# Differential attention in a hybrid diffusion step: both softmax maps kept with queries on partitions, blended there and transposed on TensorE

## The chip, the cores and the metric

The kernel runs on one core of one Trainium2 chip. The metric is the device time of one execution in microseconds (us); the time before is the median of three runs. One more execution was recorded by the hardware profiler, and all rows below come from that one.

## What is computed (the reference, cut)

Two layers run over 640 tokens (512 latent tokens and 128 context tokens) of width 1024. Each layer projects its input once, gives the parts to three groups of heads (grouped-query attention, differential attention, a gated recurrence), and multiplies the gated results with one output matrix, followed by a layer norm. The change concerns the differential heads: 4 heads of width 64, each with two softmax maps over key width 32. Latent queries see 640 keys (128 cached, 512 latent); context queries see 128.

```python
def diff_attention(q, k, v, lam):
    scale = DIFF_QK_DIM ** -0.5
    def block(qb):
        s = jnp.einsum('bqhmd,bkhmd->bhmqk', qb, k).astype(jnp.float32) * scale
        p = jax.nn.softmax(s, axis=-1)
        a = p[:, :, 0] - lam * p[:, :, 1]
        return jnp.einsum('bhqk,bkhd->bqhd', a.astype(v.dtype), v)
    return _merge_blocks(lax.map(block, _query_blocks(q)))
# in the layer:
o_d = rms_norm(diff_attention(d_q, kd, vd, lam), subln) * (1.0 - lam_init)
out_d = o_d.reshape(b, n, DIFF_WIDTH) * jax.nn.silu(d_g)
```

## The kernel before

A layer has two parts. In the first, a Python scheduler (`drive`) weaves several streams into one program order: the input projections are the background (`bg_stream`: 14 chunks of 256 columns in the order of `ORDER`, with small modulation products between them as `MODS` says), and six foreground streams go ahead of it in the order of `PRIO` whenever they are ready. Each `yield` of a stream names a cost, as TensorE time and latency, from the table `COST`; the scheduler only uses it to choose the order. In the second part the output projection and the layer norm run.

Projections are split into high and low halves (three products for one) of type float32r; their outputs are written to a pool of 49 buffers of 128x640 float32 (`gran`, `GRAN = 49`), which nearly all large tiles of the layer share. PSUM is divided into banks by use: two for projections (A), three for transposed scores, transposes and small things (B), one for attention outputs (O), and one double bank for forward scores (S).

The attention heads go through three foreground streams. `prep_stream` (`diff_prep`, L1104) rotates, transposes and splits queries and keys, and lays them out by DMA as operand tiles `QD` and `KD` of 96 rows for one map of one head; `ahead` and the constant `LOOK` limit how far it may run ahead. `sp_stream` (L639) makes the forward pass `s_pass` (L1010) for two items at a time, where an item is one map of one head: for each of 4 query tiles, scores with queries on partitions into the S bank (L1023), the row maximum on VectorE (L1030), the exponential in place with the row sum on ScalarE (L1031). Only the maximum and the sum are kept: `finish_m` makes one offset for each row, a small product turns it (L1039), and ScalarE writes it into additional rows of the query operand (L1042). `SPA` limits how many passes run ahead of the values. `pv_stream` (L650) then computes the scores again, transposed, with keys on partitions (`st_tile`, L1082, the offset included as additional rows of the contraction), takes the exponential (L1088), and multiplies the result with the values (`pv_steps`, L1146; plain float32, two heads beside each other in the output's rows). For the differential heads this is done for map 0 and for map 1, and VectorE blends the two outputs (L1166). The 128 context queries take the same way in `s_ctx`, `st_ctx` and `diff_pv_ctx` (L1168). The grouped-query heads use the same functions with `two=True`.

The recurrence (`hgrn_pair`) copies blocks of its matrices out of PSUM, those of width 32 on ScalarE (L925) and those of width 64 on VectorE (L927).

Of the kernel before, what the change touches and what calls it, by code (L numbers as in the profile page):

```python
# [39 lines left out]
LOOK = (0, 1)  # L40
PEND = 0
SPA = (2, 3)
# [5 lines left out]
COST = (dict(mod=(0.43, 2.59), norm0=(0.0, 4.0), norm1=(0.4, 0.96), gmix=(0.35, 21.63), h_exp=(0.06, 2.01),  # L48
              h_diag=(2.13, 0.37), h_lvl=(0.0, 3.0), h_mm=(0.99, 0.0), h_kst=(0.0, 1.4), h_tr=(0.0, 0.0),
              h_u=(7.96, 1.11), h_out=(22.66, 1.86), s_max=(0.0, 1.59), s_tr=(0.0, 0.2), c_max=(0.44, 3.0),  # L50
              c_tr=(1.29, 0.0), d_rq=(0.0, 1.96), d_rk=(0.53, 1.34), d_spl=(0.77, 1.91), d_tr=(4.22, 0.0),
              d_ctx=(0.72, 1.8), pv_c=(0.3, 0.3), g_ss=(0.0, 1.28), g_rope=(0.0, 2.5), g_k=(0.0, 0.71),
              g_ctx=(0.0, 1.2), g_spl=(0.0, 0.87), g_tr=(1.22, 2.24), pv_c2=(4.13, 5.2), s_g=(0.49, 1.79),
              s_d=(0.38, 1.88), pv_e=(0.77, 0.7), pv_g=(1.3, 0.56), pv_d=(1.04, 0.21)),
        dict(mod=(1.04, 9.27), norm0=(0.36, 5.34), norm1=(0.0, 0.68), gmix=(0.15, 21.63), h_exp=(0.0, 1.75),
              h_diag=(1.09, 1.27), h_lvl=(0.0, 3.0), h_mm=(0.89, 0.0), h_kst=(0.0, 1.63), h_tr=(0.0, 0.0),
              h_u=(7.96, 1.11), h_out=(22.66, 2.33), s_max=(0.3, 1.59), s_tr=(0.0, 0.19), c_max=(0.36, 3.68),
              c_tr=(1.29, 0.0), d_rq=(0.0, 1.96), d_rk=(0.53, 1.34), d_spl=(0.72, 1.39), d_tr=(2.29, 0.0),
              d_ctx=(0.6, 1.8), pv_c=(0.0, 0.28), g_ss=(0.0, 1.28), g_rope=(1.04, 4.49), g_k=(0.0, 0.71),
              g_ctx=(0.0, 1.2), g_spl=(0.07, 0.35), g_tr=(1.22, 2.24), pv_c2=(4.13, 5.4), s_g=(0.34, 2.27),  # L60
              s_d=(0.37, 1.67), pv_e=(0.77, 0.97), pv_g=(1.3, 0.44), pv_d=(0.86, 1.01)))
# [12 lines left out]
def hybrid_kernel(ctx: ExitStack, tc: tile.TileContext, A, cst, outs):  # L74
# [36 lines left out]
    def bankB():  # L111
        return bank("B")
# [410 lines left out]
    def layer(l, hT, first, defer):  # L523
# [115 lines left out]
        def sp_stream():  # L639
            for j in range(8):  # L640
                yield lambda: j < SPA[l] or ("pv", j - SPA[l]) in done
                yield from s_pass(2 * j, items, prog, j >= 4)
                done.add(("sp", j))
                if j % 2:
                    yield from s_ctx(2 * j - 2, items, j >= 4)
                    done.add(("spc", j))
# [3 lines left out]
        def pv_stream():  # L650
            for j in range(8):
                yield has(("sp", j))
                it = items[2 * j:2 * j + 2]
                if j < 4:
                    if j % 2 == 0:
                        outs[j] = outs[j + 1] = gran(name="of")
                    yield from diff_pv(l, j % 2, it, nlam, outs[j])
                else:
                    outs[j] = gran(name="mf")
                    yield from gqa_pv(j // 2 - 2, it, outs[j])  # L660
                done.add(("pv", j))
                if j % 2:
                    yield has(("spc", j))
                    it = items[2 * j - 2:2 * j + 2]
                    if j < 4:
                        yield from diff_pv_ctx(l, it, nlam, outs[j])
# [175 lines left out]
    def hgrn_pair(l, p, q, G, Kk, rv, out):  # L842
# [167 lines left out]
    def s_pass(n0, items, prog, two):  # L1010
        nmx = small.tile([128, 4, 2], F32, tag="nmx", name="nmx")
        den = small.tile([128, 4, 2], F32, tag="den", name="den")
        K1 = slice(0, 128) if two else slice(0, 96)
        off = 64 if two else 96
        for i in range(2):
            yield lambda: len(items) > n0 + i
            it = items[n0 + i]
            for t in range(4):
                ps = bankS()
                ql = it["q1"][K1, 128 * t:128 * t + 128]  # L1020
                for h in range(2):
                    c = slice(320 * h, 320 * h + 320)
                    mm(out=ps[:, h, 0:320], lhsT=ql, rhs=it["k1"][K1, c], start=True, stop=not two)  # L1023
                if two:
                    for h in range(2):
                        c = slice(320 * h, 320 * h + 320)
# [428 lines left out]
```

## Time and profile before

| | before |
|---|---|
| median of 3 runs | 952.72 us (952.4 to 954.18) |
| the profiled execution, as timed | 954.79 us |
| its span, first to last instruction | 953.0 us |
| TensorE, matmul busy | 901.2 us (95%) |
| VectorE busy | 596.5 us (63%) |
| ScalarE busy | 582.1 us (61%) |
| GpSimd busy | 79.3 us (8%) |
| attention part of layer 0, output part, attention part of layer 1 (about) | 75 to 438, 438 to 520, 520 to 890 us |

Busy is the time in which at least one instruction of the engine runs; matmuls are pipelined, and one starts while the one before it still drains. In the rows, PE is TensorE, PEld its weight loads, DVE VectorE, ACT ScalarE, POOL GpSimd, SPq the queue that issues DMAs; L1023 is line 1023 of the kernel before. Tiles are named as in the program (pS, pB, pO, pA are PSUM banks).

### The profile page before, as it was taken

How to read it: one execution, taken by the hardware profiler on the slowest of the kernel's cores; microseconds unless marked ns; L12 is line 12 of the kernel's file. 1: busy time of each engine (PE TensorE's matmuls, PEld its weight loads, DVE VectorE, ACT ScalarE, POOL GpSimd, SP SyncE). 2: the span in 40 equal slices, each digit the busy share in tenths (PEclk: the TensorE clock that was granted, in tenths of full speed). 3: DMA queues.
4: the chain of work that ended last, by engine and by line, in shares of the span. 5: the costliest groups of instructions: out<-in, count | busy, mean ns of one | idle time of the engine just before them, and what ended most of it. 6: DMA issues, size and time to landing. Idle time of an engine off the chain costs nothing.

```text
span 953.0 us, 20559 instructions
## 1 busy us (share of the span) xinstructions
PE 901.2 (95%) x8213; PEld 749.7 (79%) x8213; DVE 596.5 (63%) x1340; ACT 582.1 (61%) x1309; POOL 79.3 (8%) x113
## 2 busy tenths in 40 slices
PE   6999999999999999999999999999989989999995
PEld 3798877887777758678989997878768867777895
DVE  2355557756777865343697466785587795544467
ACT  2335677567776867773265368656877676877311
POOL 0000002000001010200023000020000100210012
PEclk8899999999999999999999999999999999999998
DMA  9946521344431212215614452114124122114222
GB/s 291 315 139 177 150 88 37 104 138 112 128 92 53 91 32 69 70 51 186 208 67 151 114 153 86 29 45 120 51 78 122 47 69 54 51 45 133 77 91 99
DMA packets 103617, 100.37 MB, mean 105 GB/s; under 512 B 9449, under 2 KB 91873, under 8 KB 103521
## 3 DMA queue, kind: packets, MB, share of 16 engines
q1 hardware_dynamic: 103520, 99.05, 35.0%
q8 instruction: 65, 1.06, 0.5%
q14 instruction: 32, 0.25, 0.1%
HBM read 77.25 MB, written 6.31 MB: 88 GB/s over the span
## 4 chain that ended last, share of the span: by engine, by line
PE 70%; DVE 12%; ACT 7%; DMA 7%; issue 2%; SPq 1%; POOL 0%; DVEq 0%; ACTq 0%; POOLq 0%
PE pA L373 8%; PE pA L375 8%; PE pA L374 8%; PE pO L1146 7%; PE pA L394 5%; PE pS L1023 5%; PE pA L395 5%; PE pA L396 5%; DMA wraw<-in_w_in_dram 4%; DMA Q<-Q 2%; PE pS L1027 2%; PE pB L1082 2%; PE pB L1080 2%; PE pB L1079 2%; ACT pS L1031 1%
## 5 line engine op out<-in xcount | busy, mean ns | idle before, releaser
L1030 DVE TENSOR_REDUCE nmx<-pS 128x1 f32<-128x640 f32 x128 | 105.4, 823 | 119.9 <-PE pS L1023 65.3
L373 PE MATMUL pA<-wh,mh 128*128 128x256 f32 x600 | 171.0, 285 | 1.3 <-DVE gate_t L409 1.3
L375 PE MATMUL pA<-wh,ml 128*128 128x256 f32 x600 | 170.3, 284 | 0.0
L374 PE MATMUL pA<-wl,mh 128*128 128x256 f32 x600 | 170.0, 284 | 0.0
L1031 ACT ACTIVATE pS<-pS,nmx 128x640 f32<-128x640 f32 x128 | 98.2, 767 | 50.4 <-DVE nmx L1030 47.5
L260 ACT CAST wh<-wraw 128x512 fp32r<-128x512 f32 x140 | 83.7, 619 | 73.4 <-PE pA L375 31.9
L261 DVE TENSOR_TENSOR wl<-wraw,wh 128x512 fp32r<-128x512 f32 x140 | 92.8, 689 | 39.8 <-ACT wh L260 39.0
L373 PEld LDWEIGHTS pA<-wh,mh 128*128 128x128 f32 x600 | 114.7, 191 | 3.6 <-DVE gate_t L409 2.0
L375 PEld LDWEIGHTS pA<-wh,ml 128*128 128x128 f32 x600 | 114.6, 191 | 1.7 <-issue 1.2
L374 PEld LDWEIGHTS pA<-wl,mh 128*128 128x128 f32 x600 | 114.7, 191 | 1.1 <-issue 0.8
L1088 ACT ACTIVATE PT<-pB 128x512 f32<-128x512 f32 x160 | 89.1, 599 | 27.0 <-PE pB L1080 14.7
L394 PE MATMUL pA<-mh,wh 128*128 128x320 f32 x224 | 71.6, 320 | 0.0
L394 PE MATMUL pA<-hh,wh 128*128 128x320 f32 x224 | 70.6, 315 | 0.7 <-DVE gate_t L409 0.7
L395 PE MATMUL pA<-ml,wh 128*128 128x320 f32 x224 | 70.8, 316 | 0.0
L396 PE MATMUL pA<-mh,wl 128*128 128x320 f32 x224 | 70.6, 315 | 0.0
L396 PE MATMUL pA<-hh,wl 128*128 128x320 f32 x224 | 69.7, 311 | 0.0
L395 PE MATMUL pA<-hl,wh 128*128 128x320 f32 x224 | 69.5, 310 | 0.0
L1146 PE MATMUL pO<-PT,tk 128*64 128x512 f32 x256 | 64.9, 613 | 0.4 <-ACT PT L1088 0.3
L373 PE MATMUL pA<-wh,hh 128*128 128x256 f32 x200 | 57.6, 288 | 0.0
L375 PE MATMUL pA<-wh,hl 128*128 128x256 f32 x200 | 57.0, 285 | 0.0
L374 PE MATMUL pA<-wl,hh 128*128 128x256 f32 x200 | 56.8, 284 | 0.0
L394 PEld LDWEIGHTS pA<-mh,wh 128*128 128x128 f32 x224 | 43.2, 193 | 2.5 <-issue 1.8
(297 smaller groups left out, 1966.3 us busy)
## 6 DMA issues: line engine op xcount, KB each, us to landing
wraw<-in_w_ada_dram SPq DMA_DIRECT2D x32, 512.0 KB, 4.5
wraw<-in_w_in_dram SPq DMA_DIRECT2D x30, 512.0 KB, 4.6
wraw<-in_w_in_dram SPq DMA_DIRECT2D x48, 256.0 KB, 3.4
wa<-in_w_ada_dram SPq DMA_DIRECT2D x32, 256.0 KB, 5.4
wraw<-in_w_out_dram SPq DMA_DIRECT2D x16, 512.0 KB, 3.5
Q<-Q SPq DMA_DIRECT2D x32, 160.0 KB, 2.6
KD<-dkh SPq DMA_DIRECT2D x32, 96.0 KB, 3.2
QD<-dqh SPq DMA_DIRECT2D x32, 80.0 KB, 3.2
```

The lines of the kernel that those rows point to most:

```text
L260: nc.scalar.copy(hi[n], src)
L261: tt(out=lo[n], in0=src, in1=hi[n].bitcast(F32), op=ALU.subtract)
L373: mm(out=ps[:, o:o + 256], lhsT=hi[k][:, sl], rhs=a, start=(n == 0), stop=False)
L374: mm(out=ps[:, o:o + 256], lhsT=hi[k][:, sl], rhs=b, start=False, stop=False)
L375: mm(out=ps[:, o:o + 256], lhsT=lo[k][:, sl], rhs=a, start=False, stop=(n == last))
L394: mm(out=ps, lhsT=wa, rhs=hi[k][:, sl], start=(k == 0), stop=False)
L395: mm(out=ps, lhsT=wa, rhs=lo[k][:, sl], start=False, stop=False)
L396: mm(out=ps, lhsT=wb, rhs=hi[k][:, sl], start=False, stop=(k == KB - 1))
L1030: dve.tensor_reduce(out=nmx[:, t, i:i + 1], in_=sv, axis=AX.XY, op=ALU.max, negate=True)
L1031: act(sv, sv, AF.Exp, bias=nmx[:, t, i:i + 1], accum_out=den[:, t, i:i + 1])
L1088: return pt, act(pt, ps, AF.Exp).ins
L1146: x = mm(out=o[64 * (i % 2):64 * (i % 2) + 64], lhsT=value(k, i % 2), rhs=pt, start=k == 0, stop=k == 4)
```

## The change

The differential heads no longer compute their scores twice. `d_pass` takes both maps of one head: scores with queries on partitions as before, but the exponential is written to a kept tile `P` of 128x640 in SBUF. For each query tile map 1 is scaled by the row factor -lambda x (sum of map 0) / (sum of map 1) and added to map 0 on VectorE. When both heads of a pair are blended, `turn_maps` transposes the blended map in 128x128 blocks on TensorE, ScalarE copies four of them out of PSUM at a time, and the values are multiplied once for each head. The remaining factor, 1 / (sum of map 0) for each query, is broadcast, transposed likewise, and multiplied onto the output. The context queries go the same way (`d_ctx`, `diff_pv_ctx`). The additional rows of the operands, their memsets and the writes of turned maxima are dropped for these heads; the grouped-query heads keep theirs. The recurrence's 64-wide blocks are copied on ScalarE too. The constants of the scheduler (`LOOK`, `SPA`, `PRIO`, `ORDER`, `MODS`, `COST`) are set anew; the changes of `COST` are left out here.

```diff
-LOOK = (0, 1)
+LOOK = (1, 2)
-SPA = (2, 3)
+SPA = (3, 5)
...
-PRIO = ((1, 0, 2, 3, 5, 4), (0, 5, 1, 2, 3, 4))
-ORDER = ((0, 1, 4, 3, 2, 5, 6, 8, 7, 9, 10, 11, 12, 13),
-         (0, 1, 3, 2, 4, 5, 7, 6, 8, 9, 10, 11, 12, 13))
+PRIO = ((2, 3, 4, 1, 0, 5), (0, 5, 1, 2, 3, 4))
+ORDER = ((0, 1, 4, 3, 2, 5, 6, 7, 8, 9, 10, 11, 12, 13),
+         (1, 0, 3, 4, 2, 5, 7, 6, 8, 9, 10, 11, 12, 13))
...
-        {0: (8,), 3: (9,), 9: (10,), 10: (11,)})
+        {2: (8,), 3: (9,), 9: (10,), 10: (11,)})
...
-                yield from s_pass(2 * j, items, prog, j >= 4)
+                yield from s_pass(2 * j, items, prog) if j >= 4 else d_pass(2 * j, items, prog, nlam)
...
             for j in range(8):
+                if j in (0, 2):
+                    continue
                 yield has(("sp", j))
-                it = items[2 * j:2 * j + 2]
+                it = items[4 * (j // 2):4 * (j // 2) + 4]
                 if j < 4:
-                    if j % 2 == 0:
-                        outs[j] = outs[j + 1] = gran(name="of")
-                    yield from diff_pv(l, j % 2, it, nlam, outs[j])
+                    outs[j - 1] = gran(name="of")
+                    yield from diff_pv(it, outs[j - 1])
+                    done.add(("pv", j - 1))
...
-                        if m == 32:
-                            nc.scalar.copy(o, v[r])
-                        else:
-                            dve.tensor_copy(o, v[r])
+                        nc.scalar.copy(o, v[r])
...
+    def map_tile(it, t, den):
+        ps = bankS()
+        for h in range(2):
+            mm(out=ps[:, h, 0:320], lhsT=it["q1"][0:96, 128 * t:128 * t + 128],
+               rhs=it["k1"][0:96, 320 * h:320 * h + 320], start=True, stop=True)
+        nmx = small.tile([128, 1], F32, tag="nmd", name="nmd", bufs=4)
+        sv = ps[:, :, 0:320]
+        dve.tensor_reduce(out=nmx, in_=sv, axis=AX.XY, op=ALU.max, negate=True)
+        P = gran(name="P")
+        act(P.rearrange("p (h k) -> p h k", h=2), sv, AF.Exp, bias=nmx, accum_out=den)
+        return P
+
+    def d_pass(n0, items, prog, nlam):
+        den = small.tile([128, 2, 4], F32, tag="dend", name="dend", bufs=2)
+        rd = small.tile([128, 2, 4], F32, tag="rdd", name="rdd", bufs=4)
+        rat = small.tile([128, 4], F32, tag="rat", name="rat")
+        yield lambda: len(items) > n0 + 1
+        maps = []
+        for t0 in (0, 2):
+            late = []
+            for t in (t0, t0 + 1):
+                maps.append(map_tile(items[n0], t, den[:, 0, t:t + 1]))
+                yield cost["s_d"]
+                late.append(map_tile(items[n0 + 1], t, den[:, 1, t:t + 1]))
+                yield cost["s_d"]
+            ts = slice(t0, t0 + 2)
+            dve.reciprocal(rd[:, :, ts], den[:, :, ts])
+            stt(out=rat[:, ts], in0=rd[:, 1, ts], scalar=nlam, in1=den[:, 0, ts], op0=ALU.mult, op1=ALU.mult)
+            for t, b in zip((t0, t0 + 1), late):
+                stt(out=maps[t], in0=b, scalar=rat[:, t:t + 1], in1=maps[t], op0=ALU.mult, op1=ALU.add)
+            prog[0] = n0 + 1 + t0 // 2
+        items[n0].update(maps=maps, rd=rd[:, 0])
+        yield cost["s_max"]
...
+    def turn_maps(maps):
+        ps = bankB()
+        n = 128 * len(maps)
+        for i, x in enumerate(maps):
+            nc.tensor.transpose(ps[:, 128 * i:128 * i + 128], x, ident)
+        pt = gran((128, n), name="PT")
+        return pt, nc.scalar.copy(pt, ps[:, 0:n]).ins
...
-            yield ahead(4 * p + n)
-            i = 2 * (n % 2) + n // 2
-            r = slice(32 * i, 32 * i + 32)
+            yield ahead(4 * p + n - n % 2)
+            r = slice(32 * n, 32 * n + 32)
...
-            nc.gpsimd.memset(it["k1"][96:104].bitcast(F32), 1.0)
...
+    def diff_pv(items, of):
         dv, cv = items[0]["v"]
+        pair = (items[0], items[2])
+        rb = gran((128, 4, 2, 64), name="rb")
+        for e, it in enumerate(pair):
+            nc.scalar.copy(rb[:, :, e], it["rd"].unsqueeze(2).to_broadcast([128, 4, 64]))
+        ps = bankC()
+        for t in range(4):
+            nc.tensor.transpose(ps[:, 128 * t:128 * t + 128], rb[:, t].rearrange("p e d -> p (e d)"), ident)
+        r = gran((128, 512), name="rows")
+        nc.scalar.copy(r, ps)
         o = bankO()
...
+        def made(e, kt):
+            return turn_maps([x[:, 128 * kt:128 * kt + 128] for x in pair[e]["maps"]])
+
+        yield from pv_steps(made, value, o, "pv_d")
+        tt(out=of[:, 0:512], in0=o, in1=r, op=ALU.mult)
```

`d_ctx` does for the 128 context queries what `map_tile` and `d_pass` do for the others (four exponentials into one tile `P`, two small blends), and `diff_pv_ctx` transposes two blocks and one broadcast of row factors for each pair of heads, multiplies with the values of both heads, and scales.

## Rows read from the trace of the kernel before

**Rows 1.** The page's engine line: busy us (share of the span) xinstructions.
```profile
PE 901.2 (95%) x8213; PEld 749.7 (79%) x8213; DVE 596.5 (63%) x1340; ACT 582.1 (61%) x1309; POOL 79.3 (8%) x113
```

**Rows 2.** Table of stretches: stretch, its length, busy us by engine, granted clock, DMA.
```profile
75.00:438.00 363.00, 348.92 (x3329) 275.66 (x3329) 226.17 (x476) 251.92 (x566) 26.96 (x36) 1.00 0.34 97
110.00:270.00 160.00, 153.84 (x1572) 122.20 (x1572) 106.19 (x226) 108.28 (x247) 11.32 (x17) 1.00 0.37 103
520.00:890.00 370.00, 355.51 (x3350) 293.42 (x3350) 232.83 (x468) 254.91 (x570) 25.81 (x36) 0.99 0.29 82
```

**Rows 3.** The chain that ended last, by engine (the page's part 4).
```profile
PE 70%; DVE 12%; ACT 7%; DMA 7%; issue 2%; SPq 1%; POOL 0%; DVEq 0%; ACTq 0%; POOLq 0%
```

**Rows 4.** TensorE's waits: waiter <- releaser: us in total, times, longest.
```profile
PE pB L1067 <- DVE mhc L1008: 3.8, 3, 1.6
...
PE pO L1146 <- ACT PT L1088: 0.5, 2, 0.3
```

**Rows 5.** Timeline, two forward score tiles in a row: start us, length us, instruction.
```profile
90.33 0.46 PE L1023 MATMUL pS<-KD,QD 96*128 96x320 f32 x2
...
92.63 0.56 PE L1023 MATMUL pS<-KD,QD 96*128 96x320 f32 x2
```

**Rows 6.** TensorE's groups by shape: xcount | busy us, mean ns | idle before.
```profile
L1082 PE MATMUL pB<-QD,KD 100*128 100x512 f32 x80 | 30.5, 430 | 2.8 <-ACT PT L1088 1.9 <-ACT QD L1042 0.6
...
L1101 PE MATMUL pB<-cs,tk 128*128 128x128 f32 x90 | 14.7, 279 | 0.4 <-DVE tk L448 0.3
```

**Rows 7.** TensorE's timeline: transposed scores (L1082) and values (L1146) among projections.
```profile
118.57 1.00 PE L1082 MATMUL pB<-QD,KD 100*128 100x512 f32 x3
119.41 0.28 PE L375 MATMUL pA<-wh,hl 128*128 128x256 f32 x1
...
119.89 0.39 PE L1082 MATMUL pB<-QD,KD 100*128 100x512 f32 x1
120.12 0.28 PE L373 MATMUL pA<-wh,hh 128*128 128x256 f32 x1
...
120.80 1.08 PE L1146 MATMUL pO<-PT,dcv 128*64 128x512 f32 x4
121.71 1.03 PE L1146 MATMUL pO<-PT,tk 128*64 128x512 f32 x4
122.67 0.56 PE L1023 MATMUL pS<-KD,QD 96*128 96x320 f32 x2
```

**Rows 8.** TensorE's timeline: context scores (L1055) and turned maxima (L1039).
```profile
247.58 0.23 PE L1055 MATMUL pS<-KD,QD 96*128 96x128 f32 x1
247.69 0.41 PE L1039 MATMUL pB<-identr,mhl 128*4 128x128 f32 x4
247.93 0.49 PE L1055 MATMUL pS<-KD,QD 96*128 96x128 f32 x3
```

**Rows 9.** TensorE's timeline: four transposes of 128x128 float32 and the next instruction.
```profile
790.35 0.60 PE L961 MATMUL pB<-cs,kst 128*128 128x128 f32 x4
790.78 0.27 PE L965 MATMUL pB<-cs,kst 128*128 128x128 f32 x1
```

**Rows 10.** ScalarE's groups: exponentials of transposed scores, writes of turned maxima.
```profile
L1088 ACT ACTIVATE PT<-pB 128x512 f32<-128x512 f32 x160 | 89.1, 599 | 27.0 <-PE pB L1080 14.7 <-PE pB L1082 11.4
...
L1042 ACT ACTIVATE QD<-pB,cs 4x512 fp32r<-4x512 f32 x16 | 10.1, 671 | 7.4 <-PE pB L1039 7.3
```

**Rows 11.** VectorE's groups: row maxima, 64-wide block copies, a blend-like product of 128x640.
```profile
L1030 DVE TENSOR_REDUCE nmx<-pS 128x1 f32<-128x640 f32 x128 | 105.4, 823 | 119.9 <-PE pS L1023 65.3 <-PE pS L1027 54.0
...
L927 DVE COPY af<-pB 64x320 f32<-64x320 f32 x16 | 7.8, 487 | 2.2 <-PE pB L904 1.9
...
L568 DVE SCALAR_TENSOR_TENSOR sq<-of,sgain,sq 128x640 f32<-128x640 f32 x4 | 3.5, 881 | 1.9 <-ACT sq L567 1.9
```

**Rows 12.** Waits of the DMA queue: L94 moves query and key rows into tiles.
```profile
SPq L94 <- DVE kst L954: 14.8, 1, 14.8
```

More of the change, by code (lines that the diff above doesn't have):

```diff
@@ L1019, in s_pass @@
                 ps = bankS()
-                ql = it["q1"][K1, 128 * t:128 * t + 128]
+                ql = it["q1"][:, 128 * t:128 * t + 128]
                 for h in range(2):
                     c = slice(320 * h, 320 * h + 320)
[L1023 to L1026, printed above, removed]
-                        mm(out=ps[:, h, 0:320], lhsT=it["q2"][0:72, 128 * t:128 * t + 128], rhs=it["k2"][0:72, c],
-                           start=False, stop=True)
+                    mm(out=ps[:, h, 0:320], lhsT=ql, rhs=it["k1"][:, c], start=True, stop=False)
+                for h in range(2):
+                    c = slice(320 * h, 320 * h + 320)
+                    mm(out=ps[:, h, 0:320], lhsT=it["q2"][0:72, 128 * t:128 * t + 128], rhs=it["k2"][0:72, c],
+                       start=False, stop=True)
                 sv = ps[:, :, 0:320]
@@ L1031, in s_pass @@
                 act(sv, sv, AF.Exp, bias=nmx[:, t, i:i + 1], accum_out=den[:, t, i:i + 1])
-                yield cost["s_g" if two else "s_d"]
+                yield cost["s_g"]
             prog[0] = n0 + i + 1
@@ L1054, in s_ctx @@
             q, q2, k1, k2 = it["q1"][:, 512:640], it["q2"][:, 512:640], it["k1"][:, 640:768], it["k2"][:, 640:768]
-            mm(out=o, lhsT=q[K1], rhs=k1[K1], start=True, stop=not two)
-            if two:
-                mm(out=o, lhsT=q2[0:72], rhs=k2[0:72], start=False, stop=True)
+            mm(out=o, lhsT=q, rhs=k1, start=True, stop=False)
+            mm(out=o, lhsT=q2[0:72], rhs=k2[0:72], start=False, stop=True)
         dve.tensor_reduce(out=nmx, in_=ps[:, 0].rearrange("p (i k) -> p i k", i=4), axis=AX.X, op=ALU.max,
@@ new lines, in d_ctx @@
+    def d_ctx(n0, items, nlam):
+        nmx = small.tile([128, 4], F32, tag="nmxc", name="nmxc")
+        den = small.tile([128, 4], F32, tag="denc", name="denc")
+        rat = small.tile([128, 4], F32, tag="ratc", name="ratc")
+        yield lambda: len(items) > n0 + 3 and "ctx" in items[n0]
+        ps = bankS()
+        for i, it in enumerate(items[n0:n0 + 4]):
+            mm(out=ps[:, 0, 128 * i:128 * i + 128], lhsT=it["q1"][0:96, 512:640], rhs=it["k1"][0:96, 640:768],
+               start=True, stop=True)
+        dve.tensor_reduce(out=nmx, in_=ps[:, 0].rearrange("p (i k) -> p i k", i=4), axis=AX.X, op=ALU.max,
+                          negate=True)
+        P = gran((128, 4, 128), name="P")
+        for i in range(4):
+            act(P[:, i], ps[:, 0, 128 * i:128 * i + 128], AF.Exp, bias=nmx[:, i:i + 1], accum_out=den[:, i:i + 1])
+        dve.reciprocal(rat, den)
+        for i in range(0, 4, 2):
+            stt(out=rat[:, i + 1:i + 2], in0=rat[:, i + 1:i + 2], scalar=nlam, in1=den[:, i:i + 1], op0=ALU.mult,
+                op1=ALU.mult)
+            stt(out=P[:, i], in0=P[:, i + 1], scalar=rat[:, i + 1:i + 2], in1=P[:, i], op0=ALU.mult, op1=ALU.add)
+        items[n0]["ctx"] = (P, rat)
+        yield cost["c_max"]
@@ L1136, in diff_prep, with pv_steps @@
         out[-4]["ctx"] = True
-    def pv_steps(items, two, value, o):
+    def pv_steps(made, value, o, key):
         ready = []
         for kt in range(6):
-            now = [st_tile(items[e], kt, two) for e in range(2)] if kt < 5 else []
+            now = [made(e, kt) for e in range(2)] if kt < 5 else []
             if len(ready) == 4 or kt == 5:
@@ L1151, in pv_steps @@
             ready += now
-            yield cost["pv_e" if kt == 5 else "pv_g" if two else "pv_d"]
-    def diff_pv(l, m, items, nlam, of):
+            yield cost["pv_e" if kt == 5 else key]
+    def diff_pv(items, of):
         dv, cv = items[0]["v"]
+        pair = (items[0], items[2])
[7 more added lines that the diff above has]
+        nc.scalar.copy(r, ps)
         o = bankO()
```

92 lines of the change are left out of this document (41 added, 51 removed).

## The prediction

> **What bounds the kernel now.** I read the engine line of the page first: TensorE is busy in 95% of the span, ScalarE and VectorE in 61 and 63% [rows 1]. That is a mean over stages, so the table of stretches comes next. The change touches only the attention part of the two layers, 75 to 438 us and 520 to 890 us; there too TensorE is busy 348.9 of 363 us and 355.5 of 370 us, 96% of both, VectorE 62 and 63% [rows 2]. The reader is to see that the projections of the same layer fill whatever the attention leaves of TensorE. The chain that ended last says the same: 70% of it is TensorE work, 12% VectorE [rows 3]. And TensorE's own waits are short; of those around the attention heads, the worst is the wait of the small product that transposes the context maxima, 3.8 us in 3 waits; the value products waited for their exponentials 0.5 us in all [rows 4]. So in these stretches a matmul that goes away is time, if the next chain has room. The next chain is the score chain: one PSUM buffer, so scores, row maximum, exponential, then the next scores. Its period is 92.63 - 90.33 = 2.30 us [rows 5]; 128 tiles of it are 294 us out of 733 us of attention. It has room for more than twice its length.
>
> **How TensorE is priced.** The duration of a matmul in the groups is its latency, because matmuls overlap: 279 ns for a transpose, 430 ns for a 512-column score product [rows 6]. What it costs a full engine is the distance from its start to the next start. Three score products start at 118.57 and the next instruction at 119.41: 0.28 us each; a single one takes 120.12 - 119.89 = 0.23, and I take 0.25. Four records of the value product (two heads, two records each, since the operands are plain float32) take 121.71 - 120.80 = 0.91 and then 122.67 - 121.71 = 0.96 us: 0.93 for one key tile of two heads [rows 7]. The four small products that turn the maxima take 247.93 - 247.69 = 0.24, or 0.06 each; a context score product of 128 columns 247.69 - 247.58 = 0.11 [rows 8]. Four transposes of 128x128 float32 take 790.78 - 790.35 = 0.43, or 0.108 each [rows 9].
>
> **What TensorE loses.** In two layers there are 8 passes over a differential map pair, each with 10 transposed score products: 80 [rows 6], all gone: 80 x 0.25 = 20.0 us. The context's 16 transposed ones of 128 columns, at the 0.11 of the forward one, 1.8 us [rows 8]. The values are multiplied with one blended map instead of two, so 4 of 8 runs of 5 key tiles go: 20 x 0.93 = 18.6 us. The 32 small products that turn the maxima: 1.9 us; those of the context and half of the context's value products, about 1 us together. Sum removed: 43.3 us.
>
> **What it gains.** Each pair of heads now needs, for 5 key tiles, 2 heads and 4 query tiles, 40 transposes; 2 pairs and 2 layers make 160. The row factors are broadcast and transposed as well: 4 for each pair, 16; the context has 2 + 1 for each pair, 12. Together 188 x 0.108 = 20.3 us. The forward score products stay as they are. Net: 43.3 - 20.3 = 23 us less TensorE work.
>
> On that price one rule speaks against the change. In the trace a group of four transposes occupies TensorE for 0.43 us although each lasts 279 ns, so they overlap [rows 6, 9]. The Trainium skill ("TensorE: Matmul & The Clock Gate", Part 4, PE-mode transpose) gives about 275 ns for one transpose in a kernel and says that transposes don't hold the clock up. By 275 ns the 188 would take 52 us and the sum would turn into +8 us; the latency agrees with the trace, the price in a stream does not.
>
> **Waits.** Gone with the maxima: the context wait of the differential heads. Two of the 3 waits are theirs; the third, the longest at 1.6 us, belongs to the grouped-query heads, so 2.2 us go [rows 4]. New: the first transposes of a pair wait for the last blend, that is two products of 0.88 and some small reciprocals on VectorE behind the last exponential [rows 11], about 2.5 us of latency. Projection matmuls stand beside it and cover most; the trace of before has no such wait, so it is bounded by 0 (all covered) and 2.5 us x 4 pairs = 10 us (nothing covered). I take 4, nearer to the covered end, since the same kind of wait, exponential to value product, is covered but for 0.5 us now [rows 4]. So 23 + 2.2 - 4 = 21 us are gained.
>
> **The other engines.** ScalarE: 80 exponentials of 599 ns become 40 copies of the same shape out of PSUM, -24 us; the 16 writes of turned maxima go, -10; four copies of the output go, about -3; added are broadcast and row copies, some +6, and the 16 copies of the 64-wide recurrence blocks that come over from VectorE, at no more than their 0.49 there, +7 [rows 10, 11]. Net about -24 of 582 us. VectorE: 32 blends of 128x640 at 0.88 are +28 us [rows 11], the context's blends and reciprocals some +6; gone are the 16 block copies (-7.8) and the arithmetic on maxima and masks, about -10. Net +16 of 596 us: 64% busy, still no bound. Queued behind the blends on VectorE are the next row maximum and the low halves of the projection weights. A pass of 8 score tiles gets 4 blends, 3.5 us on 18.4 us, so the score chain grows to at most 2.7 us a tile in these stretches, and is still half of the time that it has. GpSimd loses 16 memsets and is idle anyway. The DMAs that lay out queries and keys are the same number in the same queue; they may start earlier (the look-ahead is one tile longer), and the keys' buffers come free after the forward pass instead of after the values.
>
> The retuned order of chunks moves work between neighbours but neither adds nor removes any; I cost it at nothing, covered by the fact that TensorE has something to do in 96% of either order. If that cover is gone, the price is that of a stall of a projection for a weight load, a few us.
>
> **Rivals.**
> 1. The handover binds. Both heads of a pair must be blended before the first transpose, so the value products of a pair come later and in one block of 10 steps, and the blends stand in VectorE's line. Then the uncovered end of the new wait holds (10 us in place of 4), and the score chain's growth, 64 differential tiles x 0.4 = 26 us, shows in perhaps a fifth, 5 us: 952.7 - 21 + 6 + 5 = 943. For it: the row maximum waits 65 us in total for differential and other score products already, so the two run in lockstep [rows 11]. Against: TensorE rarely waits for either of them.
> 2. More waits go than I count. TensorE idles some 28 us in the two attention parts together [rows 2]; a lighter ScalarE, fewer handovers and one pass over the values could return a third of that: 952.7 - 21 - 10 = 922.
> 3. Slower: the pool of 49 large buffers runs out. The blended maps are kept as 128x640 tiles: 8 for a pair until its values are done, up to 4 more for the next head and 4 second maps in flight, where before only 4 exponential tiles were live at once; 4 query tiles a pair come free earlier, so some 8 to 10 more of 49. That the pool is short now is visible: moves into query tiles waited 14.8 us for a buffer that the recurrence held [rows 12]. If the projections' outputs have to wait for a buffer until a pair is done, TensorE stops, since there are two PSUM banks for them. One stop would last about a run of values, 12 us; four of them make 48, and 952.7 - 21 + 48 = 980. It decides against the change from 5.3 us a pair on (21 / 4). Against: no wait of TensorE in the trace ends on such a release.
> 4. Slower: transposes don't overlap in their new place (they come behind blends and between float32 products), and cost their 279 ns [rows 6]: 188 x 0.279 = 52 us, net 52 - 43 = +9, and with the waits of the sum above +11: 964. The page of the Trainium skill named above ("TensorE: Matmul & The Clock Gate", Part 4) gives nearly that figure. Against it stand the four in 0.43 us, and the clock: the stretch from 110 to 270 us, which holds 22 transposes in such groups, ran at a granted clock of 1.00 [rows 2].
> 5. The change does less than it says: schedule and savings cancel within 0.2%, 952.
>
> **How the numbers follow.** The profiled execution took 953.0 us in its span and 954.8 as timed, 2 us above the median of 952.7; less 21 that execution would be 933.6, and against the median it is 931.5; I give 931. Chances: forecast 0.62 (926 to 937), rival 1 0.13, rival 2 0.12, rival 3 0.08, rival 4 0.02, rival 5 0.03. The range for 8 in 10 takes in rivals 1 and 2 with a margin for the bounds of the new wait: 916 to 946. A measurement of this kernel can tell about 0.2% (2 us) from no change: faster 0.87, same 0.03, slower 0.10.
>
> **What would show it.** Right: the transposed score products of the differential heads are gone, 80 fewer records of value products, some 188 transposes whose groups of four stand 0.43 us apart, TensorE's busy time down by over 20 us at an unchanged 95% share, VectorE up by about 16 us and ScalarE down by about 24. Rival 1 would show as idle time of TensorE before the map transposes, released by VectorE; rival 3 as projection matmuls that wait for an evacuation which waits for a buffer; rival 4 as groups of four that take over 1 us, or as a lower granted clock in 110 to 270 us and 570 to 725 us. The prediction is wrong if TensorE's busy time falls by 20 us and the time does not: then the score chain, not TensorE, set the pace.

## The result and the profile after

The changed kernel takes 961.4 us (median, 960.5 to 963.8), the kernel before, on the same chip, 953.1 us: a ratio of 1.0086, interval 1.0072 to 1.0101. It is 8 us slower, where 931 us and a gain of 21 had been forecast. The range of 916 to 946 us does not hold it.

| | before | after |
|---|---|---|
| median | 953.1 us | 961.4 us |
| span of the profiled execution | 953.0 us | 958.8 us |
| TensorE busy | 901.2 us | 885.2 us |
| rest of the span, TensorE not busy | 51.8 us | 73.6 us |
| mean granted clock of TensorE | 0.984 | 0.969 |
| VectorE / ScalarE busy | 596.5 / 582.1 us | 612.4 / 556.5 us |

The engine line of the changed kernel's page (columns as in [rows 1]):

```profile
PE 885.2 (92%) x8173; PEld 752.3 (78%) x8173; DVE 612.4 (64%) x1360; ACT 556.5 (58%) x1265; POOL 68.2 (7%) x97
```

Against [rows 1], TensorE's busy time fell by 16.0 us, ScalarE's by 25.6, VectorE's rose by 15.9. The work went where the sum had put it. But the span grew, so the time in which TensorE does nothing grew by 73.6 - 51.8 = 21.8 us. The second loss is the clock. The records know two levels, 2.4 and 1.2 GHz (1.00 and 0.50 in the rows), so a mean of 0.969 means that 2 x 0.031 x 958.8 = 59 us of the span lay at 1.2 GHz, against 2 x 0.016 x 953.0 = 30 us before. The table of stretches shows where (columns as in [rows 2]; the last two stretches are 3 and 4 us long):

```profile
75.00:438.00 363.00, 335.79 (x3287) 278.22 (x3287) 235.29 (x486) 238.44 (x539) 24.78 (x32) 0.97 0.32 91
110.00:270.00 160.00, 144.57 (x1562) 127.24 (x1554) 113.48 (x231) 92.25 (x215) 8.55 (x13) 0.95 0.39 109
520.00:890.00 370.00, 349.14 (x3338) 293.62 (x3337) 237.63 (x474) 239.82 (x547) 22.86 (x32) 0.97 0.30 84
...
214.30:217.50 3.20, 3.20 (x16) 3.20 (x16) 2.08 (x5) 2.12 (x6) 0.00 (x0) 0.50 0.00 0
218.00:222.00 4.00, 4.00 (x31) 4.00 (x31) 3.41 (x8) 1.83 (x6) 0.00 (x0) 1.00 0.42 131
```

From 110 to 270 us TensorE was busy for 153.8 us before [rows 2] and for 144.6 now, and the clock fell from 1.00 to 0.95. Full stretches look like 218 to 222 us: 31 matmuls in 4 us. From 214.3 to 217.5 us the same kind of work runs at half the clock, 16 matmuls in 3.2 us. What stands ahead of such a stretch is in the list of TensorE's waits (waiter <- releaser: us in total, times, longest):

```profile
PE pS L1090 <- ACT P L1096: 11.2, 9, 2.3
PE pA L394 <- DVE gate_t L409: 5.6, 2, 4.2
PE pS L1019 <- ACT pS L1026: 3.4, 7, 1.7
```

L1090 is the score product of a differential tile; it waits for the PSUM bank that the exponential of the tile before it (L1096) still reads. That is the score chain of [rows 5], no longer beside other work. L1019 and L1026 are the same for the grouped-query heads. In the kernel before, one line serves both groups of heads, and its wait is a small one in the list of [rows 4]:

```profile
PE pS L1023 <- ACT pS L1031: 2.7, 6, 0.8
```

So the waits for a score chain rose from 2.7 to 14.6 us. Those of L394 on L409 rose from 0.7 to 5.6 us. The two together are 17 of the 21.8 us; the rest is the balance of many short waits. TensorE's timeline shows one such place, in layer 1 (start us, length us, instruction, in brackets the idle time before it and what ended it):

```profile
639.34 0.66 PE L1147 MATMUL pB<-cs,P 128*128 128x128 f32 x4 [0.30 <-ACT af L925]
639.75 0.37 PE L375 MATMUL pA<-wh,ml 128*128 128x256 f32 x1
639.96 0.46 PE L1090 MATMUL pS<-KD,QD 96*128 96x320 f32 x2
642.31 0.56 PE L1090 MATMUL pS<-KD,QD 96*128 96x320 f32 x2 [1.89 <-ACT P L1096]
644.71 0.90 PE L1090 MATMUL pS<-KD,QD 96*128 96x320 f32 x2 [1.84 <-ACT P L1096]
645.40 1.05 PE L1147 MATMUL pB<-cs,P 128*128 128x128 f32 x4
```

Three score tiles follow each other with nothing between. Each takes its whole chain, 642.31 - 639.96 = 2.35 and 2.40 us, and TensorE stands still for 1.89 and 1.84 us of it. The four transposes at 639.34 last 0.66 us from the first start to the last end; those at 645.40, after the two idle stretches, last 1.05 us. The score products at 644.71 last 0.90 us, those at 642.31, which also come behind a wait, 0.56: that is the lower clock. The same happens at 209 to 214 us, with five short products between the first two of three tiles, just ahead of the half-clock stretch above.

In all, seven stretches at the low clock lie in the two attention parts now (from about 88, 142, 214, 252, 555, 644 and 736 us), 3 to 10 us long and 44 us together; before there were three, 14 us together. Each of the seven begins during idle time of TensorE of 1.2 us or more, or right behind it. Four of them (214, 252, 644 and 736) stand at waits for a score chain, the last of these in the grouped-query heads.

The wait on L409 has a like cause. At 85.67 us a score tile stands right ahead of a projection product that needs a PSUM bank (here with ScalarE and VectorE, left out the weight loads):

```profile
85.67 0.53 PE L1090 MATMUL pS<-KD,QD 96*128 96x320 f32 x2
86.63 0.82 DVE L1094 TENSOR_REDUCE nmd<-pS 128x1 f32<-128x640 f32 x1
87.48 0.79 ACT L1096 ACTIVATE P<-pS,nmd 128x640 f32<-128x640 f32 x1 [2.08 <-DVE nmd L1094]
...
88.27 0.43 ACT L406 ACTIVATE sge<-pA 128x320 f32<-128x320 f32 x1
...
89.32 0.47 ACT L408 ACTIVATE sge<-sge 128x320 f32<-128x320 f32 x1
89.82 0.49 DVE L409 TENSOR_TENSOR gate_t<-pA,sge 128x320 f32<-128x320 f32 x1 [2.37 <-ACT sge L408]
...
90.37 0.63 PE L394 MATMUL pA<-hh,wh 128*128 128x320 f32 x1 [4.16 <-DVE gate_t L409]
```

ScalarE waits 2.08 us for the row maximum before it takes the exponential, and the evacuation of the projection (L406, L408) is queued behind that. TensorE idles for 4.16 us.

### The profile page after: what moved, and what is told of

Its sections match the earlier page's. It is cut to its first block, busy times and chain, and to the rows that moved or that the text cites. A ratio compares the mean times of both kernels' runs of the same rounds, so it can differ in the third digit from the quotient of the medians.

```text
span 958.8 us, 20346 instructions
## 1 busy us (share of the span) xinstructions
PE 885.2 (92%) x8173; PEld 752.3 (78%) x8173; DVE 612.4 (64%) x1360; ACT 556.5 (58%) x1265; POOL 68.2 (7%) x97
## 3 DMA queue, kind: packets, MB, share of 16 engines
q8 instruction: 64, 1.05, 0.5%
## 4 chain that ended last, share of the span: by engine, by line
PE 68%; DVE 12%; ACT 10%; DMA 5%; issue 3%; SPq 1%; POOL 0%; DVEq 0%; ACTq 0%; POOLq 0%
PE pA L373 8%; PE pA L375 8%; PE pA L374 8%; PE pA L394 5%; PE pA L396 5%; PE pO L1196 5%; PE pA L395 5%; DMA wraw<-in_w_in_dram 3%; PE pS L1090 2%; PE pS L1019 2%; PE pB L1071 2%; PE pS L1022 2%; ACT wh L260 2%; DVE wl L261 2%; PE pB L1070 2%
## 5 line engine op out<-in xcount | busy, mean ns | idle before, releaser
L373 PE MATMUL pA<-wh,mh 128*128 128x256 f32 x600 | 173.6, 289 | 4.6 <-ACT tk L414 1.8
L261 DVE TENSOR_TENSOR wl<-wraw,wh 128x512 fp32r<-128x512 f32 x140 | 95.9, 714 | 41.1 <-ACT wh L260 39.6
L1096 ACT ACTIVATE P<-pS,nmd 128x640 f32<-128x640 f32 x64 | 50.8, 794 | 63.8 <-DVE nmd L1094 63.0
L1094 DVE TENSOR_REDUCE nmd<-pS 128x1 f32<-128x640 f32 x64 | 52.6, 822 | 55.1 <-PE pS L1090 54.8
L1025 DVE TENSOR_REDUCE nmx<-pS 128x1 f32<-128x640 f32 x64 | 52.5, 821 | 52.4 <-PE pS L1022 51.9
L394 PE MATMUL pA<-hh,wh 128*128 128x320 f32 x224 | 72.3, 323 | 6.8 <-DVE gate_t L409 5.6
L394 PE MATMUL pA<-mh,wh 128*128 128x320 f32 x224 | 71.5, 319 | 2.7 <-ACT tk L414 1.4
L373 PE MATMUL pA<-wh,hh 128*128 128x256 f32 x200 | 59.8, 299 | 3.0 <-issue 3.0
L1026 ACT ACTIVATE pS<-pS,nmx 128x640 f32<-128x640 f32 x64 | 49.1, 767 | 19.0 <-DVE nmx L1025 16.7
L1077 ACT ACTIVATE PT<-pB 128x512 f32<-128x512 f32 x80 | 44.8, 600 | 10.2 <-PE pB L1071 9.9
```

Of the source, the lines that this page charges most:

```text
L261: tt(out=lo[n], in0=src, in1=hi[n].bitcast(F32), op=ALU.subtract)
L373: mm(out=ps[:, o:o + 256], lhsT=hi[k][:, sl], rhs=a, start=(n == 0), stop=False)
L394: mm(out=ps, lhsT=wa, rhs=hi[k][:, sl], start=(k == 0), stop=False)
L1025: dve.tensor_reduce(out=nmx[:, t, i:i + 1], in_=sv, axis=AX.XY, op=ALU.max, negate=True)
L1026: act(sv, sv, AF.Exp, bias=nmx[:, t, i:i + 1], accum_out=den[:, t, i:i + 1])
L1094: dve.tensor_reduce(out=nmx, in_=sv, axis=AX.XY, op=ALU.max, negate=True)
```

## The experiments

Two theories were to be told apart. A: the order of instructions leaves differential score tiles without cover, and the saving of TensorE work is lost in the chain of scores, row maximum and exponential. B: the new work itself costs the time (blends, handover, transposes, buffers, ScalarE's additional copies). All ratios are against the kernel before on the same chip in the same job.

| kernel | median | ratio, interval | TensorE not busy | mean clock |
|---|---|---|---|---|
| before | 953.1 | 1 | 51.8 | 0.984 |
| after | 961.4 | 1.0086 (1.0072 to 1.0101) | 73.6 | 0.969 |
| e1 new code, old constants | 1001.1 | 1.0497 (1.0468 to 1.0526) | 94.6 | 0.949 |
| e2 old code, new constants | 993.5 | 1.0422 (1.0388 to 1.0456) | 76.0 | 0.964 |
| e3 layout costs nothing | 966.1 | 1.0126 (1.0099 to 1.0152) | 77.8 | 0.969 |
| e4 47 buffers | 962.7 | 1.0100 (1.0069 to 1.0131) | 75.7 | 0.969 |
| e5 no row maximum | 938.5 | 0.9844 (0.9819 to 0.9868) | 59.7 | 0.983 |
| e6 no blend | 951.3 | 0.9972 (0.9954 to 0.9990) | 69.3 | 0.968 |
| e7 transposes twice | 980.8 | 1.0294 (1.0264 to 1.0324) | 73.3 | 0.969 |
| e8 blocks on VectorE | 967.8 | 1.0152 (1.0132 to 1.0173) | 81.2 | 0.969 |
| e9 old code, no row maximum | 947.8 | 0.9925 (0.9904 to 0.9946) | 51.1 | 0.986 |
| e10 new code, other order | 953.7 | 1.0001 (0.9977 to 1.0025) | 70.0 | 0.972 |
| e11 e10 without row maximum | 945.6 | 0.9911 (0.9880 to 0.9942) | 56.7 | 0.973 |
| e12 new code, other order, all work | 954.9 | 0.9995 (0.9978 to 1.0012) | 71.7 | 0.968 |

Not busy is the span less TensorE's busy time. The last two columns are of one execution of each kernel, the profiled one; that of e10 took 957.4 and that of e12 957.9 us, 3 to 4 us over their medians, that of e11 941.0, 5 under. The order of instructions is made anew for each kernel, so an edit can also move instructions that it does not name: in the traces of e5, e6 and e8 about a tenth of TensorE's records stand in another place of its order than in that of after. Differences of a few us between two kernels need not be the price of the edit.

**e1 and e2: code and constants crossed.** e1 is the changed code with the scheduler's constants of before, e2 the code of before with the new constants.

```diff
# e1, in the changed kernel (e2 the other way round)
-LOOK = (1, 2)
-SPA = (3, 5)
+LOOK = (0, 1)
+SPA = (2, 3)
...
-PRIO = ((2, 3, 4, 1, 0, 5), (0, 5, 1, 2, 3, 4))
+PRIO = ((1, 0, 2, 3, 5, 4), (0, 5, 1, 2, 3, 4))
```

> The changed code with the scheduler's constants of the kernel before (LOOK, SPA, PRIO, ORDER, MODS, COST), nothing else. Theory A (TensorE got its 22 us less work, but the order of instructions leaves score tiles without projection work between them, so TensorE idles and its clock falls): the constants decide as much as the operations, and these were not set for the new steps: 965 to 985 us. Theory B (the new operations themselves, blends on VectorE and transposes, cost the time wherever they stand): the constants matter little, 956 to 966 us.

> The code before with the changed kernel's constants. Theory A: the old code loses as well when its order is changed, with more idle time of TensorE and more low clock, 962 to 980 us. Theory B: close to the kernel before, 951 to 957 us, since no new operation is in it.

e1 took 1001.1 us, e2 993.5 us; both lie above every expectation (at most 985 and 980). With the old constants the new code costs 48 us, with the new constants it saves 32 us (993.5 to 961.4). So "the change" cannot be priced apart from the order: the constants move the time by 40 us either way, about twice the TensorE work that the change saves. In e2, whose arithmetic is that of before, the largest wait is the score chain (columns as above):

```profile
PE pS L1023 <- ACT pS L1031: 19.5, 16, 1.9
```

In the kernel before it was 2.7 us in 6 waits; an order made for other work uncovers the same chain. What e1 loses is mostly something else: L1090 waits there 6.8 us for L1096, less than the 11.2 in after. Against after, TensorE is idle 21 us longer, in many places, and busy 22 us longer (907.3 to 885.2) at a mean clock of 0.949.

**e3: the layout steps cost nothing.** The scheduler holds that a step which only issues layout DMAs (`d_tr`) takes 4.22 and 2.29 us of TensorE, so it lets the next score tile follow it without a projection between.

```diff
-... d_tr=(4.22, 0.0) ...   ... d_tr=(2.29, 0.0) ...
+... d_tr=(0.0, 0.0) ...    ... d_tr=(0.0, 0.0) ...
```

> The changed kernel, but the scheduler's cost d_tr of laying out one item by DMA is 0 us of TensorE time instead of 4.22 and 2.29, so that two layouts no longer let the scheduler believe that TensorE was busy between two score tiles. Theory A: the runs of uncovered score tiles near 209 and 640 us go; if they are the main loss 950 to 957 us, and if the order is spoilt elsewhere instead 958 to 970 us with the idle time at other places. Theory B: 959 to 964 us.

It took 966.1 us, 5 us more than after and in the range given for an order that is spoilt elsewhere; the wait of L1090 on L1096 grew from 11.2 us (9 times) to 15.4 us (13 times). Mending this one cost moved the bare tiles to other places. That this entry alone is the fault fell.

**e4: two buffers fewer.** `GRAN = 49` becomes 47.

> The changed kernel with 47 instead of 49 of the large buffers. Theory C (the kept maps exhaust the pool, projections wait for buffers): slower by 10 us or more, 972 us or over. Theories A and B: the pool has room, 959 to 965 us.

962.7 against 961.4 us, within the measurement. If the pool were short, two buffers fewer would show. Rival 3 falls.

**e5 and e9: no row maximum.** The row maximum of the differential tiles is left out; the exponential is taken of the scores as they are. The softmax is the same in exact arithmetic, but nothing guards against an overflow any more.

```diff
# e5, changed kernel
-        nmx = small.tile([128, 1], F32, tag="nmd", name="nmd", bufs=4)
-        dve.tensor_reduce(out=nmx, in_=sv, axis=AX.XY, op=ALU.max, negate=True)
-        act(P.rearrange("p (h k) -> p h k", h=2), sv, AF.Exp, bias=nmx, accum_out=den)
+        act(P.rearrange("p (h k) -> p h k", h=2), sv, AF.Exp, accum_out=den)
# e9, kernel before
+        if not two:
+            nc.gpsimd.memset(nmx, 0.0)
...
-                dve.tensor_reduce(out=nmx[:, t, i:i + 1], ...)
+                if two:
+                    dve.tensor_reduce(out=nmx[:, t, i:i + 1], ...)
```

> The changed kernel without the row maximum of the differential score tiles: the exponential is taken of the scaled scores as they are (the 64 reductions of 128x640 on VectorE are left out; the ratio of the maps stays the same in exact arithmetic). TensorE's work stays as it is. Theory A (the time went into score tiles that follow each other with too little projection work between them, so that scores, row maximum, exponential are seen one after the other): the chain of a tile loses the 0.8 us of its reduction, the bare tiles give back most of their 10.8 us and some low-clock stretches go: 944 to 953 us. Theory B (TensorE is the bound also in the new order, and what was lost was lost elsewhere, in the projections' own waits): 957 to 962 us.

> The kernel before, with the row maximum of the differential score tiles left out in the same way: 64 reductions of 128x640 are replaced by a memset to zero on GpSimd in each pass, and the offset is the logarithm of the sum alone. Theory A (in the old order nearly every differential score tile had projection work beside it, so its chain was covered; only the new order shows it): 944 to 951 us, a third or less of the 23 us that the same edit gave to the changed kernel. Theory B (64 reductions fewer on VectorE give about 20 us to any order, so the changed kernel lost its time elsewhere): 930 to 938 us.

e5 took 938.5 us, 23 less than after and below both ranges; e9 947.8 us, 6.8 less than before (954.5 in its job), inside that of A. TensorE has the same work in each pair, and VectorE loses the same 64 reductions. In the old order that is worth a third of what it is worth in the new one. TensorE's idle time says why: it fell by 13.9 us from after to e5 and by 0.7 from before to e9. There the chain was covered, here it is not. (What e9 gains is nearly all busy time, 901.2 to 895.9 us; why stays open.) Of the 13.9 us, 6.5 are the wait of L1090 (11.2 to 4.7) and 2.8 that of L394 on L409 (5.6 to 2.8); how much of the rest comes from the shorter chain, from a VectorE with less to do, or from the moved order stays open. The engine line and stretches of e5:

```profile
PE 874.1 (94%) x8173; PEld 746.6 (80%) x8173; DVE 565.8 (61%) x1296; ACT 550.3 (59%) x1265; POOL 68.1 (7%) x97
```

```profile
75.00:438.00 363.00, 343.96 (x3396) 285.57 (x3394) 216.13 (x460) 238.43 (x546) 24.76 (x32) 0.99 0.35 100
520.00:890.00 370.00, 353.47 (x3412) 299.43 (x3411) 225.11 (x460) 240.16 (x549) 23.05 (x32) 0.99 0.30 86
```

The clock is back at 0.99 in both, though every transpose is still there. And the same place of the program as at 640 us above, three score tiles in a row:

```profile
623.96 0.45 PE L1090 MATMUL pS<-KD,QD 96*128 96x320 f32 x2
...
625.36 0.56 PE L1090 MATMUL pS<-KD,QD 96*128 96x320 f32 x2 [0.94 <-ACT P L1094]
...
626.79 0.56 PE L1090 MATMUL pS<-KD,QD 96*128 96x320 f32 x2 [0.88 <-ACT P L1094]
```

The period is 1.40 and 1.43 us in place of 2.35 and 2.40, and the idle time half. Low clock follows here too, behind one more wait of 1.08 us, but it lasts half as long: about 7 us in after, about 3 in e5 (columns as in [rows 2], first after, then e5):

```profile
644.50:651.00 6.50, 5.84 (x16) 2.55 (x16) 3.19 (x7) 5.21 (x14) 0.00 (x0) 0.50 0.42 95
628.60:631.80 3.20, 2.79 (x8) 0.77 (x8) 0.92 (x3) 2.83 (x8) 0.00 (x0) 0.50 0.52 124
```

The books of the pair after and e5: span 958.8 - 933.8 = 25 us; TensorE not busy 73.6 - 59.7 = 13.9 us less, and its busy time 885.2 - 874.1 = 11.1 us less with the same 8173 matmuls. The clock can account for that: 59 us at 1.2 GHz became 32, and half of the difference is 13.5.

**e6: no blend.** The 32 blends are cut to one column of 640; 31 of 32 parts of that arithmetic are left out.

```diff
-                stt(out=maps[t], in0=b, scalar=rat[:, t:t + 1], in1=maps[t], op0=ALU.mult, op1=ALU.add)
+                stt(out=maps[t][:, 0:1], in0=b[:, 0:1], scalar=rat[:, t:t + 1], in1=maps[t][:, 0:1], ...)
```

> The changed kernel with the blends cut to one column of 640 (31 of 32 parts of this arithmetic are left out, 32 products of 0.9 us on VectorE); order and everything else stay. Theory A (bare score tiles): the blends stand only between one pair of query tiles and the next, the time falls by 1 to 6 us: 955 to 960. Theory B (the handover binds: blends on VectorE hold up the row maxima behind them and the transposes): 32 x 0.7 us of latency would be seen for the most part: 938 to 950.

951.3 us, 10 less than after: between the two expectations. 32 x (880 - 215) ns = 21 us of VectorE are gone, and half of it shows. The blends stand ahead of the next row maximum in VectorE's line, so they lengthen the same chain; the trace of after has such a place:

```profile
204.34 0.46 PE L1090 MATMUL pS<-KD,QD 96*128 96x320 f32 x2
...
205.60 1.68 DVE L1116 SCALAR_TENSOR_TENSOR P<-P,rat 128x640 f32<-128x640 f32 x2
207.20 0.82 DVE L1094 TENSOR_REDUCE nmd<-pS 128x1 f32<-128x640 f32 x1
...
208.99 0.56 PE L1090 MATMUL pS<-KD,QD 96*128 96x320 f32 x2 [0.71 <-ACT P L1096]
```

The scores are there at 204.80; their maximum starts 2.40 us later, behind two blends, and TensorE then stands still for 0.71 us. In e6 the wait of L1090 fell from 11.2 to 7.3 us. The clock stayed at 0.968. This is the part of B (rival 1, second half) that is real, of the size of the whole loss against before. It is no bound of its own: with the blends in place e5 is 13 us faster than e6.

**e7: transposes twice.**

```diff
-        for i, x in enumerate(maps):
-            nc.tensor.transpose(ps[:, 128 * i:128 * i + 128], x, ident)
+        for x in (maps, maps):
+            for i in range(len(maps)):
+                nc.tensor.transpose(ps[:, 128 * i:128 * i + 128], x[i], ident)
```

> The changed kernel with each of the 160 map transposes made twice into the same place, which adds 160 transposes to TensorE and nothing to other engines. If a transpose costs what the trace of before gave for a stream (0.108 us) and TensorE is the bound where they stand: +17 us, 976 to 980. If the idle time of the new order takes some of them in: 962 to 972. If they cost their latency of 0.28 us (they do not overlap): +45, about 1005.

980.8 us, 19.3 more than after and just over the 976 to 980 for the price in a stream. The line also serves the context, so 168 transposes were added: 0.115 us each. The groups of the changed kernel, before the doubling, say why their latency is no price (columns as in [rows 6]):

```profile
L1147 PE MATMUL pB<-cs,P 128*128 128x128 f32 x168 | 23.8, 282 | 0.7 <-ACT af L925 0.6
```

282 ns from start to end, 0.115 in a stream. Rival 4 falls. And nothing of the added work vanished in idle time: where transposes stand, TensorE is the bound, so the idle time is elsewhere.

**e8: the recurrence's 64-wide blocks on VectorE again.**

```diff
-                        nc.scalar.copy(o, v[r])
+                        (nc.scalar.copy if m == 32 else dve.tensor_copy)(o, v[r])
```

> The changed kernel with the recurrence's 64-wide blocks copied on VectorE again, as before the change: 16 copies of 0.49 us leave ScalarE's line and stand in VectorE's. If ScalarE's line is what the projections' first instructions wait for (evacuation behind the exponential): 954 to 958. If it is the order of score tiles alone: 959 to 963.

967.8 us, 6 more than after and above both expectations. The wait of L1090 rose to 14.1 us, that of L394 on L409 to 8.5 us. Moving these copies to ScalarE was right for the new kernel: 8 us more in VectorE's line lengthen the chain that binds. How much of the 6 us is that and how much another order stays open.

**e10, e11 and e12: another order for the same code.** The constants (costs, look-ahead, priorities, order of the chunks) were set to other values, chosen so that fewer of TensorE's instructions wait. In e10 and e11 the first two chunks of the projection in layer 0 stand in swapped places, so the work is the same but their columns of data are exchanged; in e12 they are not. The cut shows e10; e12 has `SPA = (3, 3)`, and some of its other values differ from those of e10.

```diff
-LOOK = (1, 2)
-SPA = (3, 5)
+LOOK = (1, 3)
+SPA = (4, 3)
...
-PRIO = ((2, 3, 4, 1, 0, 5), (0, 5, 1, 2, 3, 4))
+PRIO = ((3, 2, 4, 1, 5, 0), (0, 1, 2, 4, 3, 5))
```

> The changed kernel, its arithmetic untouched, with other values for the scheduler's constants (costs, priorities, look-ahead, order of the chunks), chosen so that fewer instructions of TensorE have to wait. TensorE's work, the row maxima and the blends stay. Theory A (the change's saving of TensorE work is real and was lost in the order): 940 to 950 us, below the kernel before. Theory B (maps kept with queries on partitions make a chain of scores, row maximum, exponential and blend that no order can cover): 956 to 964 us.

> The kernel of e10 without the row maximum of the differential score tiles (64 reductions left out, as in e5). If the order of e10 covers the score chain better than that of the changed kernel, the same edit gives less than the 23 us that it gave there: 4 to 12 us below e10, 930 to 942. If e10's order does not cover it: 20 us or more below e10.

> The changed kernel, nothing left out and nothing swapped, with scheduler constants close to those of e10. If e10 reached the kernel before by its order alone: 946 to 956 us, 5 to 15 below the changed kernel. If the swapped columns of e10 had made its time: 958 to 965.

e10 took 953.7 us, e12 954.9 us, 7.8 and 6.5 less than after and, against the kernel before, 1.0001 and 0.9995 with intervals that hold 1. So the order alone returns what the change had lost, with every blend, row maximum and transpose in place; that speaks against B. But 940 to 950 had been expected, so A's strong form, that another order makes the whole saving visible, missed too. TensorE's idle time hardly fell: none of the five orders of the changed code with all its work (after, e1, e3, e10, e12) has less than 70 us of it, where the kernel before has 51.8. The wait of L1090 on L1096 fell in e12 from 11.2 to 6.0 us; others rose:

```profile
PE pA L394 <- DVE gate_t L409: 9.4, 2, 5.2
PE pS L1090 <- ACT P L1096: 6.0, 6, 2.2
PE pS L1090 <- DMA KD<-dkl: 4.4, 3, 3.6
```

e11 is 8.1 us below e10 (the same edit gave 23 in the order of the change, 7 in that of before). That is inside the 4 to 12 expected if the order covers more of the chain, though 945.6 us is above the 930 to 942 that went with it. The profiled executions do not bear that reading out: TensorE's idle time fell by 13.3 us (70.0 to 56.7), about as much as in e5. What did not come back is the clock, 0.972 and 0.973. The same three tiles of layer 1, with idle times of 0.95 and 0.89 us and one of 1.08 behind them, nearly the same as in e5, are followed here by 13.5 us at half the clock:

```profile
625.50:639.00 13.50, 12.42 (x71) 7.35 (x71) 4.81 (x9) 8.11 (x20) 0.00 (x0) 0.50 0.17 40
```

Neither e10 nor e11 nor e12 beats e5. Whether some order gives the changed code the full 22 us stays open; e9 and e5 are the fairest pair here for the change itself: with a short score chain on both sides the new code is 9 us faster, 938.5 to 947.8, and its TensorE busy time is 21.8 us lower (895.9 to 874.1). Even there less than half of the saved work shows in the time; TensorE's idle time is 8.6 us longer (51.1 to 59.7).

## Why the prediction was wrong

- **The net of TensorE's terms held.** The forecast was a net of 23 us less work. Busy time fell by 16.0 us while some 29 us more lay at 1.2 GHz, which stretches busy time; in the pair e9 and e5, whose clocks are nearly equal, it falls by 21.8 us. Of the single terms only the price of a transpose was tried: 0.108 us in the forecast, 0.115 in e7. The Trainium skill ("TensorE: Matmul & The Clock Gate", Part 4, PE-mode transpose) gives about 275 ns for one transpose in a kernel. An estimate by that figure makes e7 some 46 us slower; it was 19.3, and the 282 ns in the trace agree with the figure as the latency.
- **The other engines held.** ScalarE -25.6 (forecast -24), VectorE +15.9 (forecast +16).
- **The step that failed** is the one that cost the retuned order at nothing, "covered by the fact that TensorE has something to do in 96% of either order". With it fell "a matmul that goes away is time, if the next chain has room": TensorE's idle time rose by 21.8 us, as much as the work that went. The 96% are a mean of the old order [rows 2]. They say that there was cover for the score tiles where that order had put them, not that there is cover in any order. The price named for a lost cover, "a few us", comes from no row. e1 and e2 put the price of an unfit order at 40 us each (1001.1 to 961.4, 993.5 to 953.8 in its job), twice the saving; e10 and e12 put that of the order which came with the change at 7 to 8 us against another one.
- **The next chain was sized wrongly.** "It has room for more than twice its length" was a sum over 733 us; what counts is each place by itself. A differential tile took 2.35 to 2.40 us from start to start where it stood bare, close to the 2.30 of [rows 5], so its length was right. The chain's own wait in the kernel before, 2.7 us, was passed over in the reading of [rows 4]. With 43 us of products gone between the tiles, and transposes of only 20 put elsewhere, there is less beside it: three tiles follow each other in each layer with nothing or little between.
- **The new wait for the blends** was bounded by 0 and 2.5 us a pair. TensorE's waits of transposes are small: 0.7 us ahead of L1147, most of it for copies of the recurrence, and 1.3 us ahead of L1212, the transposes of the row factors. What the blends cost came by another way: e6 shows 10 us, at least in part since they stand ahead of the next row maximum on VectorE. The prediction had that in rival 1, at 5 us ("perhaps a fifth" of 26), and of its two halves the handover hardly shows and the chain was twice as dear.
- **Rivals.** 1 was right in kind by its second half, but gave 943: it had neither the tiles left bare by the order nor the clock. 2 (more waits go) is refuted by 73.6 us of TensorE not busy. 3 by e4. 4 by e7; the low clock that it names in 110 to 270 us did come (0.95), but behind idle TensorE, and in e5, with all transposes in place, that stretch is at 0.99. 5 is nearest in size and describes e10 and e12. None of the five had slower by way of the order.
- **The last sentence** of the prediction, that the score chain sets the pace if TensorE's busy time falls and the time does not, is what e5 and e9 show for the places where its tiles stand bare; over the whole span TensorE is still busy in 92%.

What the sum should have held: idle time of TensorE up by 21.8 us, and 59 - 30 = 29 us more at half clock. Set against 22 us of work, that gives a loss of up to 14 us if all those 29 us were busy ones (half of 29, plus 21.8, less 22), and none if they were idle; measured were 5.8 us of span between the two profiled executions.

## What to carry to other kernels

A busy share of 96% says that a latency chain is covered in the order that was measured, and is no promise for another one: when a change alters the order or thins out the work between links of a chain, list the places where two links would follow each other with less work between than the chain's period, and price each at the period less that work. Work taken from a busy engine need not show in the time while the chain beside it keeps its length: here 22 us of it gave nothing in the best order tried, and 9 us once the chain was shortened on both sides. 0.8 us less in each link of the chain was worth 23 us in the new order and 7 in the old. Cross the code and the tuned constants before judging either: each of the two sets fits its own code better than the other's.

## What was not expected of the hardware

The low clock comes after stalls that look harmless. At 642.3 and 644.7 us TensorE had stood still for 1.89 and 1.84 us with one score tile between, and from there the two products of a score tile last 0.90 us in place of 0.56; at 214.3 us, after 1.25 and 1.83 us of idleness on either side of a score tile, 3.2 us of dense matmuls ran at a granted clock of 0.50 and 16 matmuls were done where 25 fit at 1.00. So an idle microsecond of a full engine can cost more than itself: in the pair after and e5 13.9 us of TensorE not busy went together with 11.1 us of shorter busy time for the same 8173 matmuls. It is no fixed price: from e10 to e11 13.3 us less of idle time went together with only 3.2 us of shorter busy time, and behind nearly the same three waits the clock stayed low for about 3 us in e5 and about 14 in e11. What makes that difference is not shown.
